# SwiGLU gate and up with the tokens held in the array and 512 weight columns streamed, on one Trainium2 core

## The chip, the core and the metric

The kernel runs as one program on one core of a Trainium2 chip. The metric is the device time of that core in microseconds, the median of several runs. PE is the matrix engine, DVE the vector engine, ACT the engine for activation functions, SP the queue that issues the loads. SBUF is the on-chip memory of 128 partitions in which an operand has a byte address within its partition; PSUM is the accumulator memory of eight banks of 512 float32 per partition.

## The reference, cut to what matters

Two layers of a decoder trunk on 256 tokens of width 2048, in float32. Layer 0 mixes by latent attention and a gated delta rule, layer 1 by RWKV-7 time mixing. Each mixer is followed by a SwiGLU network between two norms:

```
h = h + rms_norm(mixer(rms_norm(h)))
h = h + rms_norm(swiglu(rms_norm(h)))
swiglu(x) = (silu(x @ w_gate) * (x @ w_up)) @ w_down      # 2048 -> 5632 -> 2048
```

## The kernel before, in words

**Split products.** PE multiplies in a reduced-precision float32 type (fp32r), so every operand is split in two: `hi` is a rounded copy made by ACT and `lo` the rest, made by DVE (`split`, L268 to L270). A product is the sum of three matmuls, hi·hi, hi·lo and lo·hi (`mm3`, L311; the matmuls have the lines L313, L315 and L316 in the wide form, L313, L318 and L319 in the other).

**Weights** come from DRAM in chunks of 128 partitions × 1024 columns (two rows of blocks of 512 columns), 512 KB each, issued by SP at L367 into three buffers `raw`. Every chunk is split into `whi` and `wlo`, also with three buffers each (`wchunks`, L291).

**Two forms of a projection.** `proj_steps` (L338) holds a 128×128 block of the weight in the array and streams the 256 tokens past it; the output has channels on partitions. A chunk is 24 matmuls of 256 columns. `projT_steps` (L354) holds a block of 128 tokens of `x` in the array and streams 512 weight columns past it; the output has tokens on partitions. A chunk is 12 matmuls of 512 columns. Both fill two of four PSUM banks `pw` for 512 columns of a weight, so the next projection starts in the other two.

**SwiGLU** (`ffn`, L486) walks over 11 groups of 512 hidden channels, in parts of 4, 4 and 3 groups. In each group `proj` computes the gate and then `proj` the up product, eight chunks each. The evacuation of the gate multiplies by `rs` (the norm's reciprocal root of each token, spread over all partitions) on DVE (L504) and takes silu on ACT (L505); that of up multiplies by `rs` and by the gate on DVE (L509, L510) and splits the result into `hid_h` and `hid_l` (through L269 and L270), channels on partitions, which is the form that the down product needs. After each part `projT` with `hid` in the array and `w_down` streamed gives the output by token; `Out.evac` (L450) adds the parts up, and `Out.post` (L469) applies the post norm and adds to `h`.

**Order.** The instructions are laid out on the engines by a scheduler of the build, which takes an instruction when its inputs are there by its own timing; on the chip each engine then works through its list in that order. `weave` (L321) orders the work of the mixers by planned times.

**Where operands lie.** Tiles start on multiples of 32 bytes per partition: `epst` of 16 bytes and `hpi` of 4 bytes take 32 each. The pools lie in the order in which they are opened: `cp` (constants, `rs`, `junk`, small tiles), `wp` (`raw`, `whi`, `wlo`), `xt` (`xs_hi`, `xs_lo`: the split input of every projection), then those of the phases. In layer 0 the SwiGLU's tiles lie above two pools that layer 1 has closed by then: `rp` with 3,840 bytes of constants and `xn` with 16 × 257 × 4 = 16,448 bytes. The addresses in bytes:

| tile | in the array in | address | above a multiple of 256 |
|---|---|---|---|
| `whi`, first buffer (the others follow by 4,096) | the wide form | 36,096 | 0 |
| `xs_hi` (`xs_lo` 16,384 above) | `projT` of a mixer's output | 60,672 | 0 |
| `hid_h`, layer 1 (`hid_l` 20,480 above) | `projT` of `w_down` | 136,448 | 0 |
| `hid_h`, layer 0 (`hid_l` 20,480 above) | `projT` of `w_down` | 156,736 | 64 |
| `ch` (streamed only) | - | 195,424 | 96 |

Of the kernel before, what the change touches and what calls it, by code (L numbers as in the profile page):

```python
# [11 lines left out]
F32 = mybir.dt.float32  # L12
# [19 lines left out]
def doubling_masks(n):  # L32
    """-1 on the diagonal, 1 on the blocks below it that a doubling step joins."""
    i = np.arange(n)
    out = {}
    b = 1
    while b < n:
        blk = i // b
        m = ((blk[:, None] % 2 == 1) & (blk[None, :] == blk[:, None] - 1)) * 1.0 - np.eye(n)
        out[b] = m  # L40
        b *= 2
    return out
# [57 lines left out]
def tile_trunk(ctx: ExitStack, tc: tile.TileContext, A, out, dbg=None):  # L100
# [19 lines left out]
    class Scratch:  # L120
        """A pool of 1, 2 and 4 KB slots for one phase."""
# [23 lines left out]
    class Banks:  # L145
        """The eight PSUM banks: nw for projections, m under each other tag."""
# [41 lines left out]
    # ---------------------------------------------------------------- inputs and small parameters  # L188
# [42 lines left out]
    def params(pool):  # L231
        """the other parameters by channel"""
        pr = pool.tile([P, 3, P], F32, name="pr3")
        nc.gpsimd.memset(pr, 0.0)
        nc.gpsimd.dma_start(pr[0:96, 0, :], A["gdn_conv_w"][0].rearrange("j (c p) -> (j c) p", p=P))
        nc.gpsimd.dma_start(pr[96:100, 0, :], A["mla_q_norm"].rearrange("o (c p) -> (o c) p", p=P))
        nc.gpsimd.dma_start(pr[100:104, 0, :], A["mla_kv_norm"].rearrange("o (c p) -> (o c) p", p=P))
        nc.gpsimd.dma_start(pr[104:105, 0, :], A["gdn_out_norm"])
        nc.gpsimd.dma_start(pr[0:96, 1, :], A["rwkv_mix"][0].rearrange("j (c p) -> (j c) p", p=P))
        nc.gpsimd.dma_start(pr[96:112, 1, :], A["rwkv_w0"].rearrange("o (c p) -> (o c) p", p=P))  # L240
        nc.gpsimd.dma_start(pr[112:128, 1, :], A["rwkv_a0"].rearrange("o (c p) -> (o c) p", p=P))
        for i, n in enumerate(("rwkv_k_k", "rwkv_k_a", "rwkv_ln_w", "rwkv_ln_b")):
            nc.gpsimd.dma_start(pr[16 * i : 16 * i + 16, 2, :], A[n].rearrange("o (c p) -> (o c) p", p=P))
        nc.gpsimd.dma_start(pr[64:80, 2, :], A["rwkv_r_k"][0].rearrange("(c h) n -> c (h n)", h=2))
        yield 1
        tp = pbank("pB")
        for i in range(3):
            nc.tensor.transpose(out=tp[:, i * P : (i + 1) * P], in_=pr[:, i, :], identity=C("ident"))
            nc.vector.tensor_copy(prm[:, 1 + i, :], tp[:, i * P : (i + 1) * P])
        tsc(omka, prm[:, 3, 16:32], -1.0, 1.0, ALU.mult, ALU.add)  # L250
# [4 lines left out]
    # ---------------------------------------------------------------- helpers  # L255
# [6 lines left out]
    def behind(ins, first):  # L262
        """Has ins issued after an earlier instruction of its engine."""
        if first is not None:
            tc.add_manual_dep(ins.ins, first.ins.name, NOSYNC, reason="order")
        return ins
# [5 lines left out]
    # instructions of ACT and DVE that the splits of the next weights are not to delay  # L272
# [13 lines left out]
    def ahead(fill, kb, n, ncols):  # L286
        """Loads the rows that wchunks would load next."""
        early.append(wtiles(ncols))
        fill(early[-1][0], kb, n)

    def wchunks(fill, kbs, ncols, perm=None):  # L291
        """Loads and splits rows of a weight; yields (kb, hi, lo, first, last)."""
# [18 lines left out]
    def mm3(dst, lh, ll, rh, rl, start, stop, wide):  # L311
        """Three passes of the split product; wide: the first pair is the weight's."""
# [8 lines left out]
    def weave(tasks):  # L321
        """Emits the steps of generators (start, end, steps, generator, lead) in the order of their times;
        the lead is by how many instructions the scheduler takes them earlier."""
# [14 lines left out]
    def proj_steps(fill, kbs, ncols, xh, xl, evac, perm=None):  # L338
        """Columns of w^T x, channels on partitions: evac(i, [P, 2, T], tiles in it)."""
# [14 lines left out]
    def projT_steps(fill, kbs, xh, xl, evac):  # L354
        """512 columns of x w, tokens on partitions: evac(half, [P, 512])."""
# [17 lines left out]
    def rsq(v, n):  # L373
        """v^-1/2 of a few columns, by Newton steps from a guess by the exponent."""
# [11 lines left out]
    def rsq_table():  # L386
        """Has the table of the reciprocal root loaded before it is needed."""
        return act(tiny(1), epst[:, 0:1], AF.Abs_reciprocal_sqrt)

    def col_rs(ss, n):  # L390
        """Sums of squares [P, 2, parts] by token -> rsqrt(mean + eps) [P, 2]: the table's root and one Newton step."""
        v, m, r_ = tiny(2), tiny(2), tiny(2)
# [10 lines left out]
    def spread(col, dst, tag=None):  # L403
        """dst[:, t] = the column value of token t, on every partition."""
# [8 lines left out]
    rs = cp.tile([P, T], F32, name="rs")  # L413
    junk = cp.tile([P, 512], F32, name="junk")
# [8 lines left out]
    def feed(o, col0):  # L423
        """Four chunks of h: split parts of h*w, channels on partitions; its last instructions of ACT and DVE."""
# [15 lines left out]
    class Out:  # L440
        """Output of a sub-layer by token: times the post norm's weight, and its sums of squares."""
# [27 lines left out]
        def post(self, nxt):  # L469
            """h += rms(f) * w, 512 columns at a time."""  # L470
# [15 lines left out]
    def ffn(layer, nxt):  # L486
        """SwiGLU on the split x and its post norm; nxt as in post."""
        sc = Scratch(f"ffns{layer}", 3, 7, 1)
# [6 lines left out]
        for pi, ng in enumerate(parts):  # L495
            his, los = {}, {}
            for g in range(g0, g0 + ng):
                hid_h = fp.tile([P, 4, T], F32R, tag="hidh", name=nm("hidh"), bufs=5)
                hid_l = fp.tile([P, 4, T], F32R, tag="hidl", name=nm("hidl"), bufs=5)
                sg = S([P, 4, T], "sg")  # L500

                def ev_gate(b, ps, n):
                    gt = S([P, 2, T], "gt")
                    tt(gt, ps, bc2(rs, 2), ALU.mult)  # L504
                    act(sg[:, 2 * b : 2 * b + 2, :], gt, AF.Silu)  # L505

                def ev_up(b, ps, n):
                    ut = S([P, 2, T], "ut")
                    tt(ut, ps, bc2(rs, 2), ALU.mult)  # L509
                    tt(ut, ut, sg[:, 2 * b : 2 * b + 2, :], ALU.mult)  # L510
                    split(hid_h[:, 2 * b : 2 * b + 2, :], hid_l[:, 2 * b : 2 * b + 2, :], ut)

                proj(wfill(wg, g * 512, 512), KB, 512, xa(xs_hi), xa(xs_lo), ev_gate)
                proj(wfill(wu, g * 512, 512), KB, 512, xa(xs_hi), xa(xs_lo), ev_up)
# [13 lines left out]
    # ================================================================ layer 0: MLA + gated DeltaNet  # L528
# [45 lines left out]
    def gates():  # L574
        """beta, the log decays by token and their sums within the chunks of 128"""
# [13 lines left out]
        # log1p(u) = 2 atanh(u / (2 + u))  # L589
# [23 lines left out]
    def conv_bank(which, head0, ps):  # L613
        """causal conv of two heads from one PSUM bank"""
# [11 lines left out]
    def tok4(src, tag):  # L626
        """[P ch, (u, t)] -> PSUM bank [P tok, (c, u, ch)]"""
# [23 lines left out]
    # The key norms are folded: with k = s k^, T' = D^-1 T D for D = diag(s), and E = beta s^2 T' (v / s - e^g k S).  # L651
    def gdn_head(hq):
# [18 lines left out]
        # decay matrices [j, i]  # L671
# [40 lines left out]
    def gdn_solve(hq):  # L712
# [4 lines left out]
        # (I + M)^-1 by doubling its diagonal blocks: mt = -(I + M)^T, R = T^T  # L717
# [43 lines left out]
        # outputs by token; rms over the head with the query norm folded into its epsilon  # L761
# [25 lines left out]
    # ---- MLA  # L787
# [13 lines left out]
    def angles():  # L801
        """tables of the rotary embedding and the shared key"""
# [19 lines left out]
    def lora(i, col, scale):  # L822
        """Compressed q or kv: split parts of c * w and rsqrt of the mean square, by column and spread."""
# [132 lines left out]
    # in microseconds of the projections  # L956
# [45 lines left out]
    def mixer_out(w, fo, col0, kbs=KB, first=True):  # L1002
# [14 lines left out]
        spread(col_rs(ss, D), rs)  # L1017
# [13 lines left out]
    def turn(o):  # L1031
        """Four chunks of h times the norm's weight, channels on partitions; sums of squares by token."""
# [24 lines left out]
    # ================================================================ layer 1: RWKV-7  # L1057
# [16 lines left out]
    def normed(i, hi, lo):  # L1074
        """the normed input, its step from the token before, and the first mixture: a few channel tiles after another"""
# [37 lines left out]
    def lora32(i, w, slot, func):  # L1113
        """96 columns of w^T x in float32"""
# [29 lines left out]
    def low_rank(pr2):  # L1144
        """decay, in-context rate and gate of two channel tiles from the hidden low-rank parts"""
# [24 lines left out]
        # log decay, summed from the start of each chunk of 64  # L1170
# [23 lines left out]
    # in microseconds  # L1194
# [22 lines left out]
    # keys of two heads, block-diagonal  # L1217
# [20 lines left out]
    def headsum(dst, src, hi, lo):  # L1238
        """sums over the channels of a head, of the split src"""
# [4 lines left out]
    def rec_pre(pr2):  # L1244
        """receptance and key of two channel tiles"""
# [16 lines left out]
    def rec_head(pr2, j):  # L1262
# [4 lines left out]
        # 1 / |k|^2 by one Newton step (negated), times the inverse decay  # L1267
# [31 lines left out]
        # Gram matrices [s, t] of the two heads, one above the other  # L1299
# [14 lines left out]
        # values, centred over the head, in token layout  # L1314
# [8 lines left out]
        # decayed keys in token layout  # L1323
# [6 lines left out]
        # [(i, tokens), (chunk, head, channels)] -> tokens of a head under one another  # L1330
# [9 lines left out]
    def rec_solve(c):  # L1340
        j = c % 2
        pd, KR, AB, KG, V, BT, bon = heads.pop(c)
        # the last one is a chain of its own, in the slots of the heads
# [7 lines left out]
        # inverses of the unit triangular systems: two heads by four chunks  # L1351
# [18 lines left out]
        # chunk recurrence  # L1370
# [67 lines left out]
    # The output projection takes the channels that are done while the others are in the recurrence.  # L1438
# [29 lines left out]
    # in units of the time that two channel tiles take  # L1468
# [65 lines left out]
```

## Time and profile before

| what | value |
|---|---|
| median of 3 runs | 2735.04 us (2732.78 to 2735.78) |
| span of the profiled execution | 2731.1 us |
| its own whole time | not listed beside the runs; the span is 3.9 us under their median |
| instructions | 53510 |

A line of the page's fifth part or of the view by lines reads: line, engine, operation, output<-inputs (the streamed operand first, then the one held in the array), shapes, count | busy us, mean ns of one | idle time ahead and who ended it. A line of the timeline reads: start, length, engine, line, operation, and "xN" where N instructions are merged. Matmuls overlap, so the time that a matmul costs is the distance from one start to the next, not its length.

### The profile page before, as it was taken

The numbers are of one execution on the slowest core, as the hardware profiler recorded it, in microseconds if no ns is written. First come the engines' busy times: TensorE is split into PE (matmuls) and PEld (weight loads), VectorE is DVE, ScalarE is ACT, GpSimd is POOL, SyncE is SP. The second block draws the span as 40 slices with busy tenths as digits, with TensorE's granted clock in tenths as the row PEclk, the third lists the DMA queues.
The fourth block names the chain that finished last, engine by engine and source line by source line (L and its number), as shares of the span: only waits on it lengthen the run. The fifth ranks groups of instructions, "written<-read, shape, count | busy, mean of one in ns | idle before, by whom it ended". The sixth has DMA issues, their size and how long they took to land. (4 is left out here: it accounts for less than half of the span.)

```text
span 2731.1 us, 53510 instructions
## 1 busy us (share of the span) xinstructions
PE 2670.9 (98%) x22326; PEld 2482.5 (91%) x22326; DVE 1654.9 (61%) x2557; ACT 1347.4 (49%) x2113; POOL 35.9 (1%) x99
## 2 busy tenths in 40 slices
PE   8999999999999999998999999999799999999998
PEld 8999988899899989987999999977699989998996
DVE  7866566655445554557876676766755545555555
ACT  6655455544444443444576556554544444443443
POOL 1000000000000000000000000000000000000000
PEclk9999999999999999998999999999899999999999
DMA  7434545666666666665586333533266666666664
GB/s 213 140 109 116 161 141 194 183 182 183 188 185 183 185 185 185 185 185 178 166 279 207 106 117 116 169 123 99 88 180 184 186 193 184 183 188 193 182 182 161
DMA packets 281970, 462.07 MB, mean 169 GB/s; under 512 B 24488, under 2 KB 101728, under 8 KB 280960
## 3 DMA queue, kind: packets, MB, share of 16 engines
q1 hardware_dynamic: 281344, 458.50, 55.3%
q8 instruction: 174, 2.85, 0.4%
q14 instruction: 68, 0.56, 0.1%
q0 software_dynamic: 384, 0.16, 0.0%
HBM read 442.31 MB, written 16.29 MB: 168 GB/s over the span
## 5 line engine op out<-in xcount | busy, mean ns | idle before, releaser
L270 DVE TENSOR_TENSOR wlo<-raw,whi 128x1024 fp32r<-128x1024 f32 (+1 forms) x814 | 975.0, 1200 | 855.5 <-ACT whi L269 851.4
L269 ACT ACTIVATE whi<-raw 128x1024 fp32r<-128x1024 f32 (+1 forms) x814 | 843.9, 1039 | 1057.8 <-PE pw L315 682.0
L313 PE MATMUL pw<-xs_hi,whi 128*128 128x256 f32 x3984 | 1131.4, 285 | 4.3 <-ACT xs_hi L1095 3.6
L315 PE MATMUL pw<-xs_lo,whi 128*128 128x256 f32 x3984 | 1131.9, 285 | 0.0
L316 PE MATMUL pw<-xs_hi,wlo 128*128 128x256 f32 x3984 | 1127.7, 285 | 1.7 <-DVE wlo L270 1.6
L313 PEld LDWEIGHTS pw<-xs_hi,whi 128*128 128x128 f32 x3984 | 764.7, 192 | 6.5 <-ACT xs_hi L1095 3.9
L316 PEld LDWEIGHTS pw<-xs_hi,wlo 128*128 128x128 f32 x3984 | 762.5, 192 | 4.1 <-DVE wlo L270 2.5
L315 PEld LDWEIGHTS pw<-xs_lo,whi 128*128 128x128 f32 x3984 | 764.9, 192 | 1.5 <-DVE xs_lo L1085 0.3
L319 PE MATMUL pw<-whi,hidl 128*128 128x512 f32 x704 | 276.6, 393 | 0.0
L318 PE MATMUL pw<-wlo,hidh 128*128 128x512 f32 x704 | 275.8, 392 | 0.0
L313 PE MATMUL pw<-whi,hidh 128*128 128x512 f32 x704 | 248.6, 392 | 0.0
L319 PEld LDWEIGHTS pw<-whi,hidl 128*128 128x128 f32 x704 | 132.2, 188 | 30.1
L313 PEld LDWEIGHTS pw<-whi,hidh 128*128 128x128 f32 x704 | 132.3, 188 | 29.5
L318 PEld LDWEIGHTS pw<-wlo,hidh 128*128 128x128 f32 x704 | 132.3, 188 | 29.0
L313 PE MATMUL pw<-whi,xs_hi 128*128 128x512 f32 x256 | 103.0, 417 | 3.7 <-ACT xs_hi L269 3.5
L318 PE MATMUL pw<-wlo,xs_hi 128*128 128x512 f32 x256 | 105.0, 410 | 0.0
L319 PE MATMUL pw<-whi,xs_lo 128*128 128x512 f32 x256 | 101.7, 405 | 0.0
L316 PE MATMUL pw<-xr_hi,wlo 128*128 128x256 f32 x288 | 83.3, 289 | 2.8 <-DVE wlo L270 2.7
L313 PE MATMUL pw<-xr_hi,whi 128*128 128x256 f32 x288 | 83.3, 289 | 0.1
L315 PE MATMUL pw<-xr_lo,whi 128*128 128x256 f32 x288 | 82.6, 287 | 0.0
L313 PEld LDWEIGHTS pw<-whi,xs_hi 128*128 128x128 f32 x256 | 48.9, 193 | 15.4 <-ACT xs_hi L269 4.1
L318 PEld LDWEIGHTS pw<-wlo,xs_hi 128*128 128x128 f32 x256 | 49.5, 193 | 10.5 <-issue 0.7
(670 smaller groups left out, 2754.6 us busy)
## 6 DMA issues: line engine op xcount, KB each, us to landing
raw<-in_ffn_w_gate_dram SPq DMA_DIRECT2D x176, 512.0 KB, 3.8
raw<-in_ffn_w_up_dram SPq DMA_DIRECT2D x176, 512.0 KB, 4.3
raw<-in_ffn_w_down_dram SPq DMA_DIRECT2D x176, 512.0 KB, 4.1
raw<-in_hyb_w_in_dram SPq DMA_DIRECT2D x80, 512.0 KB, 3.6
raw<-in_hyb_w_out_dram SPq DMA_DIRECT2D x32, 512.0 KB, 3.8
raw<-in_rwkv_w_v_dram SPq DMA_DIRECT2D x32, 512.0 KB, 4.2
raw<-in_rwkv_w_r_dram SPq DMA_DIRECT2D x32, 512.0 KB, 4.1
raw<-in_rwkv_w_k_dram SPq DMA_DIRECT2D x32, 512.0 KB, 3.7
```

The source lines that it names most:

```text
L269: behind(act(hi, src, AF.Copy), after[0])
L270: behind(tt(lo, src, hi.bitcast(F32), ALU.subtract), after[1])
L313: mm(dst, lhsT=lh, rhs=rh, start=start, stop=False, skip_group_check=True)
L315: mm(dst, lhsT=lh, rhs=rl, start=False, stop=False, skip_group_check=True)
L316: mm(dst, lhsT=ll, rhs=rh, start=False, stop=stop, skip_group_check=True)
L318: mm(dst, lhsT=lh, rhs=rl, start=False, stop=False, skip_group_check=True)
L319: mm(dst, lhsT=ll, rhs=rh, start=False, stop=stop, skip_group_check=True)
```

## The change

Gate and up go through `projT`: `xs_hi` and `xs_lo` are held in the array in blocks of 128 tokens, and 512 weight columns are streamed. Their outputs then have tokens on partitions, so the norm's factor is a column `rc` of two values per partition and no longer a spread row: the gate's evacuation is one ACT instruction per token block (silu with `rc` as its scale, read from PSUM), that of up one DVE instruction (`hd` = up × `rc` × gate). Eight PE transposes of 128×128 float32 per group turn `hd` back to channels on partitions, into two PSUM banks of the tags `pA` and `pB`, from which the split into `hid_h` and `hid_l` reads. `mixer_out` writes the column `rc` in place of spreading it. `rc` is a new tile of 2 float32 per partition in the pool `cp`, between `rs` and `junk`. The scratch pool of the SwiGLU has eight slots of 2 KB in place of seven and one of 4 KB. The down product, its evacuation and all else keep their code.

```diff
-    def col_rs(ss, n):
-        v, m, r_ = tiny(2), tiny(2), tiny(2)
+    def col_rs(ss, n, out=None):
+        v, m, r_ = tiny(2), tiny(2), tiny(2) if out is None else out
...
     rs = cp.tile([P, T], F32, name="rs")
+    rc = cp.tile([P, 2], F32, name="rc")
     junk = cp.tile([P, 512], F32, name="junk")
...
-        sc = Scratch(f"ffns{layer}", 3, 7, 1)
+        sc = Scratch(f"ffns{layer}", 3, 8)
...
-                sg = S([P, 4, T], "sg")
-                def ev_gate(b, ps, n):
-                    gt = S([P, 2, T], "gt")
-                    tt(gt, ps, bc2(rs, 2), ALU.mult)
-                    act(sg[:, 2 * b : 2 * b + 2, :], gt, AF.Silu)
-                def ev_up(b, ps, n):
-                    ut = S([P, 2, T], "ut")
-                    tt(ut, ps, bc2(rs, 2), ALU.mult)
-                    tt(ut, ut, sg[:, 2 * b : 2 * b + 2, :], ALU.mult)
-                    split(hid_h[:, 2 * b : 2 * b + 2, :], hid_l[:, 2 * b : 2 * b + 2, :], ut)
-                proj(wfill(wg, g * 512, 512), KB, 512, xa(xs_hi), xa(xs_lo), ev_gate)
-                proj(wfill(wu, g * 512, 512), KB, 512, xa(xs_hi), xa(xs_lo), ev_up)
+                sg = [S([P, 512], "sg") for _ in range(2)]
+                tb = []
+                def ev_gate(b, ps):
+                    act(sg[b], ps, AF.Silu, scale=rc[:, b : b + 1])
+                def ev_up(b, ps):
+                    if not tb:
+                        tb.extend(pbank() for _ in range(2))
+                    hd = S([P, 512], "hd")
+                    stt(hd, ps, rc[:, b : b + 1], sg[b], ALU.mult, ALU.mult)
+                    for j in range(4):
+                        nc.tensor.transpose(out=tb[j // 2][:, j % 2 * T + b * P : j % 2 * T + (b + 1) * P],
+                                            in_=hd[:, j * P : (j + 1) * P], identity=C("ident"))
+                projT(wfill(wg, g * 512, 512), KB, xa(xs_hi), xa(xs_lo), ev_gate)
+                projT(wfill(wu, g * 512, 512), KB, xa(xs_hi), xa(xs_lo), ev_up)
+                for u in range(2):
+                    split(hid_h[:, 2 * u : 2 * u + 2, :], hid_l[:, 2 * u : 2 * u + 2, :], pair(tb[u]))
...
-        spread(col_rs(ss, D), rs)
+        col_rs(ss, D, rc)
```

## Rows read from the trace of the kernel before

**Rows 1.** The page, parts 1 and 2: PE's busy time, and its granted clock by slice.
```profile
PE 2670.9 (98%) x22326; PEld 2482.5 (91%) x22326; DVE 1654.9 (61%) x2557; ACT 1347.4 (49%) x2113; POOL 35.9 (1%) x99
PEclk9999999999999999998999999999899999999999
```

**Rows 2.** Stretches: gate and up in layer 0, down in layer 1 (us, busy times, clock, DMA).
```profile
524.00:684.00 160.00, 160.00 (x1336) 160.00 (x1335) 83.46 (x81) 67.95 (x71) 0.00 (x0) 1.00 0.63 184
2159.20:2240.90 81.70, 81.70 (x363) 67.63 (x361) 38.23 (x33) 35.11 (x37) 0.00 (x0) 1.00 0.62 193
```

**Rows 3.** Timeline of ACT, gate and up of layer 0: splits of the first and fifth of five chunks.
```profile
535.03 1.06 ACT L269 ACTIVATE whi<-raw 128x1024 fp32r<-128x1024 f32 x1 [1.82 <-PE pw L315]
...
546.55 1.06 ACT L269 ACTIVATE whi<-raw 128x1024 fp32r<-128x1024 f32 x1 [1.82 <-PE pw L315]
```

**Rows 4.** Timeline of PE, down of layer 1: the same matmul of chunks 1 and 31.
```profile
2159.07 0.61 PE L313 MATMUL pw<-whi,hidh 128*128 128x512 f32 x2
...
2240.67 0.61 PE L313 MATMUL pw<-whi,hidh 128*128 128x512 f32 x2
```

**Rows 5.** Timeline of PE, output projection of layer 0's mixer: the same matmul of two chunks.
```profile
484.38 0.62 PE L313 MATMUL pw<-whi,xs_hi 128*128 128x512 f32 x2
...
487.10 0.62 PE L313 MATMUL pw<-whi,xs_hi 128*128 128x512 f32 x2
```

**Rows 6.** Timeline of PE, down of layer 0: the same matmul of two chunks.
```profile
768.71 0.63 PE L313 MATMUL pw<-whi,hidh 128*128 128x512 f32 x2
...
771.51 0.63 PE L313 MATMUL pw<-whi,hidh 128*128 128x512 f32 x2
```

**Rows 7.** Timeline of PE, a projection with ch streamed: two starts 24 matmuls apart.
```profile
326.04 0.28 PE L316 MATMUL pw<-ch,wlo 128*128 128x256 f32 x1
...
328.92 0.28 PE L316 MATMUL pw<-ch,wlo 128*128 128x256 f32 x1
```

**Rows 8.** DMA issues of the two weights (count, size, us to landing).
```profile
raw<-in_ffn_w_gate_dram SPq DMA_DIRECT2D x176, 512.0 KB, 3.8
raw<-in_ffn_w_up_dram SPq DMA_DIRECT2D x176, 512.0 KB, 4.3
```

**Rows 9.** Line L313: matmuls by operand (count: ns min/median/max, first and last start, forms).
```profile
L313 PE MATMUL pw<-xs_hi,whi x3984: 276/283/581, 11.4 to 2652.6; 128*128 128x256 f32 x200
L313 PE MATMUL pw<-whi,hidh x704: 389/393/398, 684.7 to 2717.6; 128*128 128x512 f32 x176
L313 PE MATMUL pw<-xr_hi,whi x288: 274/281/470, 1329.3 to 1742.3; 128*128 128x256 f32 x144
L313 PE MATMUL pw<-whi,xs_hi x256: 387/392/796, 348.2 to 1957.1; 128*128 128x512 f32 x128
L313 PE MATMUL pw<-ch,whi x112: 277/281/472, 322.9 to 425.4; 128*128 128x256 f32 x112
L313 PE MATMUL pw<-wl,whi x64: 276/280/283, 1353.0 to 1406.9; 96*128 96x256 f32 x32, 128*128 128x256 f32 x32
```

**Rows 10.** Timeline of PE: one set of four transposes of layer 0.
```profile
89.71 0.60 PE L632 MATMUL pB<-cst,vT 128*128 128x128 f32 x4
```

**Rows 11.** Line L632: the lengths of these transposes (ns min/median/max).
```profile
L632 PE MATMUL pB<-cst,vT x16: 270/272/273, 89.7 to 229.3; 128*128 128x128 f32 x16
```

**Rows 12.** The page, part 5, and view by lines: splits and evacuations.
```profile
L270 DVE TENSOR_TENSOR wlo<-raw,whi 128x1024 fp32r<-128x1024 f32 (+1 forms) x814 | 975.0, 1200 | 855.5 <-ACT whi L269 851.4
L269 ACT ACTIVATE hidh<-ut 128x512 fp32r<-128x512 f32 x44 | 27.1, 633 | 8.5 <-DVE ut L510 8.5
L463 DVE TENSOR_TENSOR fw<-pw,fw 128x512 f32<-128x512 f32 x32 | 20.7, 682 | 10.7 <-PE pw L319 10.7
L478 DVE SCALAR_TENSOR_TENSOR hA<-fw,tiny,hA 128x512 f32<-128x512 f32 x16 | 10.9, 744 | 0.1
```

**Rows 13.** Timeline, spread of rs in layer 0: DVE's two instructions, PE's four.
```profile
514.36 0.48 DVE L407 TENSOR_SCALAR junk<-cst,tiny 128x128 f32<-128x128 f32 x2
517.71 0.60 PE L410 MATMUL pA<-junk,ones 128*128 128x128 f32 x4
```

## The prediction

> **What bounds the kernel now.** I read the page first: PE is busy for 98% of the span, and its clock is granted almost throughout [rows 1]. Then the table by stretches: in gate and up as in down, PE is busy for the whole stretch at a clock of 1.00, which is the 2.4 GHz level, while DVE and ACT are near half and the loads at 184 to 193 GB/s [rows 2]. So in these stages the time is the distance from one matmul start to the next, and the timelines give it per chunk of 512 KB. Gate and up: four chunks lie between the two splits of [rows 3], (546.55 − 535.03) / 4 = 2.88 us, or 0.120 us for each of 24 matmuls of 256 columns; the columns alone would take 256 / 2.4 GHz = 0.1067. Down in layer 1: thirty chunks in 81.60 us, 2.72 us each, or 0.2267 for each of 12 matmuls of 512 columns, whose columns take 0.2133 [rows 4]. The mixer's output projection, which holds `xs` in the array and streams weights as the change will, takes 2.72 too [rows 5]. So a matmul carries 13.3 ns (32 cycles of 2.4 GHz) beyond its columns in both forms, and wider ones pay it half as often. That is what the change can win.
>
> But down in layer 0 takes 2.80 us for the same chunk [rows 6], 6.7 ns (16 cycles) more for each matmul. Its weights, buffers, widths and clock are those of layer 1; what differs is the address of the operand in the array: by the table of addresses `hid` starts 64 bytes above a multiple of 256 in layer 0 and on one in layer 1. `whi` and `xs` lie on such multiples. The streamed operand doesn't matter in this way: `ch`, 96 above, is streamed at 24 matmuls in 2.88 us [rows 7]. I read it so: an operand held in the array off its boundary costs 16 cycles more per matmul.
>
> **What the change moves without meaning to.** `rc` takes a slot of 32 bytes in `cp`, ahead of `wp` and `xt`. So `whi`, `wlo`, `xs_hi`, `xs_lo` and `hid` of layer 1 all come to lie 32 above a multiple of 256, `hid` of layer 0 96 above (the scratch pool shrinks by 2,048, which changes nothing here). No row shows an operand held at 32. The bounds: nothing (13.3 ns as now) and 24 cycles, 10 ns, if the price goes with the bytes left to the next multiple of 128 (64 bytes cost 16 cycles, 96 then 24). Between them lie 8 cycles, if it goes with the bytes past the boundary, and 16, if any offset costs the same. I take the row that is nearest, 16 cycles, 6.7 ns [rows 6].
>
> **The sum, part by part.**
> - Gate and up: 176 + 176 chunks [rows 8]. From 2.88 us to 2.80: 352 × 0.08 = −28.2 us. (Without the offset 2.72: 352 × 0.16 = −56.3.)
> - Down in layer 1: of 704 matmuls at L313 [rows 9] half, four to a chunk, 88 chunks × 0.08 = +7.0. In layer 0 nothing, as it is off the boundary already.
> - All other projections that hold weights: of 3,984 matmuls at L313 with `xs` 352 × 8 = 2,816 are gate and up; 1,168 stay, and with 288, 112 and 64 of the other operands 1,632, times three passes 4,896 [rows 9]; × 6.67 ns = +32.6. I charge it in full, since PE is busy there too [rows 1].
> - The mixers' output projections: 256 × 3 = 768 matmuls [rows 9] × 6.67 ns = +5.1.
> - Transposes: 11 groups × 8 × 2 layers = 176. Four take 0.60 us in the trace [rows 10] and one is 0.27 long [rows 11], so (0.60 − 0.27) / 3 = 0.11 each: +19.4. They lie on PE, which has no gap to hide them.
> - The spread that goes: four float32 matmuls per layer at the same 0.11 [rows 13]: −0.9.
> - Evacuation: DVE loses three instructions of 128x512 per token block and gains one like L478, 0.744; the splits read PSUM, like L463, 0.68 [rows 12]. Lighter on an engine half idle: 0. If that cover went, the weights' splits would come late, by the 0.7 us of one such instruction at most per group, 15 in all.
> - Loads: the same bytes; at the fastest pace, 2.72 us a chunk, they ask for 193 GB/s, at which down runs without a wait [rows 2]: 0. SP and POOL get no new work.
> - A new wait: a transpose needs `hd`, and the next gate's matmuls stand behind it on PE. If the scheduler puts other matmuls in between, it costs nothing. If the transposes stand right behind up's last matmul, PE waits for two of 0.744 one after the other, less what it does meanwhile: about 0.5 us, and 1.7 if a weight's split of 1.2 us [rows 12] is ahead on DVE; 12 to 38 us over 22 groups. The one like case, PE's part of the spread, starts 2.9 us after DVE's ended [rows 13], so the scheduler leaves room. I take 0.1 us per group, +2; ends 0 and 38.
>
> Sum: −28.2 + 7.0 + 32.6 + 5.1 + 19.4 − 0.9 + 2 = **+37.0 us**. The profiled span of 2731.1 is 3.9 below the median of 2735.04, which I carry along: 2735.04 + 37.0 = **2772 us**.
>
> The Trainium skill speaks against the gain itself: "TensorE: Matmul & The Clock Gate", section "Back-to-back issue gap", gives columns / 2.4 GHz + 2.5 ns for a matmul. By that an estimate of a chunk is 2.62 us in the old form and 2.59 in the new one, and the gain 352 × 0.03 = 10.6 us, less than the transposes. The trace disagrees: 2.88 and 2.72 [rows 3, 4].
>
> **The rivals.**
> - **32 bytes cost nothing.** Then only the form counts: −56.3 + 19.4 − 0.9 + 2 = −35.8, **2699 us**, faster. It is decided in SBUF, by whether the boundary that [rows 6] shows bites at 32 too; it turns the sign below about 3.3 ns per matmul. For it: no row has an operand at 32. Against it: 64 costs 6.7 ns. The Trainium skill has it this way: "SBUF — State Buffer", section "Specifications (TRN2)", gives SBUF lines of 16 bytes, and 32 and 64 are both whole lines. By that rule 64 would cost nothing either, and [rows 6] differ from it.
> - **8 cycles, in step with the offset.** Gate and up at 2.76: −42.2, the three shifted terms halved, +22.4, `hid` of layer 0 +0 to +3.5, and +20.5 for the rest: +1 to +4, **2737 us**, no change.
> - **24 cycles.** 10 ns: gate and up 2.84, −14.1; +67.1 shifted; +20.5: +73.5, **2809 us**.
> - **PE waits for `hd`** and the offset is free: −37.8 + 12 to 38, **2709 to 2735 us**. For it: PE takes its list in order. Against it: no wait of PE stands in the stretches of [rows 2], and [rows 13].
> - **The form wins only 10 us**, as the formula above has it; on rows it would take a chunk of 2.85 in the new form, against 2.72 in [rows 5]: −10.6 + 20.5, **2745 us**.
>
> **How the numbers follow.** 16 cycles: 0.42. Free: 0.27. 8 cycles: 0.19. 24 cycles: 0.05. Waits: 0.05. Small win: 0.02. A measurement tells 0.2%, 5.5 us, from no change. Faster: the free case and most of the waits, 0.30. Same: most of the 8 cycles, 0.16. Slower: the rest, 0.54. The likeliest case alone runs from 2762 (if a third of the +32.6 is hidden in the recurrence) to 2784 (with 14 us of waits). The range must take in the free case and leaves out 24 cycles and the worst waits: **2694 to 2784**.
>
> **What would show it.** In the changed trace, gate and up at 2.80 us a chunk, down at 2.80 in both layers, and projections of weights outside the SwiGLU at 24 matmuls in 3.04 us instead of 2.88; 176 transposes 0.11 apart, and no wait of PE on `hd`. If chunks of gate and up take 2.72 and the others 2.88 as before, the offset is free and I am wrong on the sign. If PE waits on `hd` by a microsecond a group, the scheduler's room was the mistake.

## The result, and the profile after

The changed kernel takes **2696.7 us** (median of 4 runs, 2692.25 to 2702.23) against 2735.05 (2732.78 to 2735.78): ratio 0.986 [0.9846, 0.9875], 38 us or 1.4% faster. The forecast was 2772 and slower; the rival "32 bytes cost nothing" had 2699. The profiled run took 2699.26 us with a span of 2697.4.

The page of the changed kernel, parts 1 and 2, answers to [rows 1]:

```profile
PE 2633.5 (98%) x18270; PEld 2279.8 (85%) x18270; DVE 1602.1 (59%) x2465; ACT 1347.7 (50%) x2111; POOL 36.2 (1%) x99
...
PEclk9999999999999999998999999999899999999999
```

PE is the bound as before, with 4,056 matmuls fewer and the clock granted almost throughout. The table by stretches, as in [rows 2] (stretch, length, busy time of PE, PEld, DVE, ACT and POOL, clock, DMA share, GB/s): gate and up in layer 0, down in layer 0, down in layer 1.

```profile
530.00:546.00 16.00, 16.00 (x73) 13.23 (x71) 8.65 (x8) 6.37 (x6) 0.00 (x0) 1.00 0.66 197
762.00:778.00 16.00, 16.00 (x72) 13.11 (x71) 7.36 (x6) 7.29 (x8) 0.00 (x0) 1.00 0.67 194
2143.00:2225.00 82.00, 82.00 (x364) 67.89 (x363) 36.78 (x30) 36.56 (x39) 0.00 (x0) 1.00 0.63 192
```

PE has no gap in any of them at the 2.4 GHz level, and the loads of gate and up keep up at 197 GB/s. So the pace of the matmuls is again the time. The timeline of ACT in gate and up of layer 0, the splits of the first and fifth of five chunks, as in [rows 3]:

```profile
532.82 1.06 ACT L269 ACTIVATE whi<-raw 128x1024 fp32r<-128x1024 f32 x1 [1.66 <-PE pw L319]
...
543.70 1.06 ACT L269 ACTIVATE whi<-raw 128x1024 fp32r<-128x1024 f32 x1 [1.66 <-PE pw L319]
```

Four chunks in 10.88 us are **2.72 us** each: neither the old 2.88 nor the forecast 2.80. The timeline of PE gives the other projections, two rows each: `ch` streamed (as [rows 7]), the mixer's output (as [rows 5]), down in layer 0 (as [rows 6]) and down in layer 1 (as [rows 4]):

```profile
326.14 0.28 PE L316 MATMUL pw<-ch,wlo 128*128 128x256 f32 x1
...
328.96 0.28 PE L316 MATMUL pw<-ch,wlo 128*128 128x256 f32 x1
...
478.84 0.62 PE L313 MATMUL pw<-whi,xs_hi 128*128 128x512 f32 x2
...
487.00 0.62 PE L313 MATMUL pw<-whi,xs_hi 128*128 128x512 f32 x2
...
756.04 0.63 PE L313 MATMUL pw<-whi,hidh 128*128 128x512 f32 x2
...
764.44 0.63 PE L313 MATMUL pw<-whi,hidh 128*128 128x512 f32 x2
...
2145.34 0.62 PE L313 MATMUL pw<-whi,hidh 128*128 128x512 f32 x2
...
2180.70 0.62 PE L313 MATMUL pw<-whi,hidh 128*128 128x512 f32 x2
```

The 24 matmuls with `ch` take 2.82 us (2.88 before), three chunks of the mixer's output 8.16 (2.72 each, as before), three of down in layer 0 8.40 (2.80, as before), thirteen of down in layer 1 35.36 (2.72, as before). `whi`, `xs` and `hid` now lie 32 bytes further on, while `ch` keeps its place at 195,424; none of these became slower, and `ch` became quicker.

Where the time went shows in the same instruction of both kernels: the last split of down in layer 0, a split in layer 1's recurrence, and the last split of down in layer 1. From the timelines of DVE, first of before, then of after:

```profile
1252.12 1.23 DVE L270 TENSOR_TENSOR wlo<-raw,whi 128x1024 fp32r<-128x1024 f32 x1 [1.57 <-ACT whi L269]
...
1959.09 1.22 DVE L270 TENSOR_TENSOR wlo<-raw,whi 128x1024 fp32r<-128x1024 f32 x1
...
2711.44 1.23 DVE L270 TENSOR_TENSOR wlo<-raw,whi 128x1024 fp32r<-128x1024 f32 x1 [1.49 <-ACT whi L269]
```

```profile
1233.46 1.23 DVE L270 TENSOR_TENSOR wlo<-raw,whi 128x1024 fp32r<-128x1024 f32 x1 [1.57 <-ACT whi L269]
...
1943.31 1.22 DVE L270 TENSOR_TENSOR wlo<-raw,whi 128x1024 fp32r<-128x1024 f32 x1
...
2677.85 1.23 DVE L270 TENSOR_TENSOR wlo<-raw,whi 128x1024 fp32r<-128x1024 f32 x1 [1.49 <-ACT whi L269]
```

The distance is −18.7 us after layer 0, −15.8 in the recurrence and −33.6 at the end. So the SwiGLU of layer 0 gave 18.7 and that of layer 1 17.8 (at 496 us, in the output projection of layer 0's mixer, the two traces agree within 0.1 us); the mixer of layer 1 between them lost 2.9. In e8 below, which differs by a factor of 0.0 in layer 0 alone and has every tile at the same address, the three lie at 1234.19, 1939.65 and 2673.14: there the two SwiGLUs gave 17.9 and 18.9 and the mixer 1.5. So the mixer's part differs by some us from one execution to the next, and no price of the change is shown in it. By the terms of the prediction without the offset, a layer is worth 176 × 0.16 − 88 × 0.11 + 0.45 = 18.9 us.

The transposes, in the timeline of PE, between two matmuls of the next gate, and the instruction that they need, in the timeline of DVE:

```profile
548.04 0.39 PE L319 MATMUL pw<-whi,xs_lo 128*128 128x512 f32 x1
548.27 0.38 PE L513 MATMUL pA<-cst,hd 128*128 128x128 f32 x2
548.49 0.38 PE L513 MATMUL pB<-cst,hd 128*128 128x128 f32 x2
548.70 0.38 PE L513 MATMUL pA<-cst,hd 128*128 128x128 f32 x2
548.92 0.38 PE L513 MATMUL pB<-cst,hd 128*128 128x128 f32 x2
549.06 0.48 PE L313 MATMUL pw<-whi,xs_hi 128*128 128x512 f32 x1
549.37 0.40 PE L318 MATMUL pw<-wlo,xs_hi 128*128 128x512 f32 x1
```

```profile
543.22 1.40 DVE L511 SCALAR_TENSOR_TENSOR hd<-pw,rc,sg 128x512 f32<-128x512 f32 x2
```

From L319 at 548.04 to L318 at 549.37 are 1.33 us. The two matmuls of 512 columns in it take 2 × 0.2267, so eight transposes take 0.877, **0.110 us each**. `hd` is ready at 544.62, 3.65 us before the first of them (3.65 to 3.79 in all 22 groups): the scheduler put more than a chunk of the next gate in between, and the transposes wait for nothing.

### The profile page after: what moved, and what is told of

Its sections match the earlier page's. It is cut to its first block, busy times and chain, and to the rows that moved or that the text cites. A ratio compares the mean times of both kernels' runs of the same rounds, so it can differ in the third digit from the quotient of the medians.

```text
span 2697.4 us, 45270 instructions
## 1 busy us (share of the span) xinstructions
PE 2633.5 (98%) x18270; PEld 2279.8 (85%) x18270; DVE 1602.1 (59%) x2465; ACT 1347.7 (50%) x2111; POOL 36.2 (1%) x99
## 4 chain that ended last, share of the span: by engine, by line
PE 91%; DMA 3%; DVE 3%; ACT 2%; issue 1%; SPq 0%; DVEq 0%; ACTq 0%
PE pw L313 26%; PE pw L318 20%; PE pw L319 20%; PE pw L316 7%; PE pw L315 6%; PE ph L1312 1%; DMA raw<-in_rwkv_w_v_dram 1%; PE pA L1240 1%; PE pC L643 1%; PE pA L643 1%; PE pC L1240 1%; DVE wlo L270 1%; PE pB L1240 1%; DMA ygs<-bon 1%; ACT whi L269 1%
## 5 line engine op out<-in xcount | busy, mean ns | idle before, releaser
L318 PE MATMUL pw<-wlo,xs_hi 128*128 128x512 f32 x1664 | 653.2, 393 | 0.3 <-DVE wlo L270 0.3
L319 PE MATMUL pw<-whi,xs_lo 128*128 128x512 f32 x1664 | 648.8, 391 | 0.0
L313 PE MATMUL pw<-whi,xs_hi 128*128 128x512 f32 x1664 | 602.1, 395 | 6.0 <-ACT xs_hi L269 4.8
L313 PEld LDWEIGHTS pw<-whi,xs_hi 128*128 128x128 f32 x1664 | 313.8, 189 | 72.0 <-ACT xs_hi L269 5.3
L318 PEld LDWEIGHTS pw<-wlo,xs_hi 128*128 128x128 f32 x1664 | 314.3, 189 | 65.3 <-DVE wlo L270 0.7
L319 PEld LDWEIGHTS pw<-whi,xs_lo 128*128 128x128 f32 x1664 | 313.1, 188 | 65.5 <-issue 0.7
L313 PE MATMUL pw<-xs_hi,whi 128*128 128x256 f32 x1168 | 334.7, 288 | 4.8 <-ACT xs_hi L1100 3.6
L315 PE MATMUL pw<-xs_lo,whi 128*128 128x256 f32 x1168 | 335.5, 288 | 0.0
L316 PE MATMUL pw<-xs_hi,wlo 128*128 128x256 f32 x1168 | 331.4, 288 | 0.0
L319 PE MATMUL pw<-whi,hidl 128*128 128x512 f32 x704 | 276.5, 393 | 0.0
L318 PE MATMUL pw<-wlo,hidh 128*128 128x512 f32 x704 | 275.8, 392 | 0.0
L313 PE MATMUL pw<-whi,hidh 128*128 128x512 f32 x704 | 250.1, 393 | 0.0
L313 PEld LDWEIGHTS pw<-xs_hi,whi 128*128 128x128 f32 x1168 | 224.5, 193 | 6.4 <-ACT xs_hi L1100 3.8
L315 PEld LDWEIGHTS pw<-xs_lo,whi 128*128 128x128 f32 x1168 | 224.8, 192 | 1.3 <-DVE xs_lo L1090 0.3
L316 PEld LDWEIGHTS pw<-xs_hi,wlo 128*128 128x128 f32 x1168 | 222.6, 192 | 1.7 <-issue 0.7
L319 PEld LDWEIGHTS pw<-whi,hidl 128*128 128x128 f32 x704 | 132.2, 188 | 29.9
L313 PEld LDWEIGHTS pw<-whi,hidh 128*128 128x128 f32 x704 | 132.3, 188 | 29.5
L318 PEld LDWEIGHTS pw<-wlo,hidh 128*128 128x128 f32 x704 | 132.3, 188 | 29.1
L313 PE MATMUL pw<-xr_hi,whi 128*128 128x256 f32 x288 | 83.8, 291 | 1.4 <-ACT whi L269 1.4
```

The costliest lines, as they stand in the source:

```text
L313: mm(dst, lhsT=lh, rhs=rh, start=start, stop=False, skip_group_check=True)
L315: mm(dst, lhsT=lh, rhs=rl, start=False, stop=False, skip_group_check=True)
L316: mm(dst, lhsT=ll, rhs=rh, start=False, stop=stop, skip_group_check=True)
L318: mm(dst, lhsT=lh, rhs=rl, start=False, stop=False, skip_group_check=True)
L319: mm(dst, lhsT=ll, rhs=rh, start=False, stop=stop, skip_group_check=True)
```

## The experiments

All edits are made to the changed kernel. "Distance" is how far `xs`, `hid` or another operand made of tokens lies above the weight `whi` that it meets in a matmul, in bytes, modulo 256; in the form with 512 columns it is the held one and `whi` the streamed one. In the changed kernel `xs` and `hid` of layer 1 have distance 0, `hid` of layer 0 64, as in the kernel before; `rc` moved `whi` and all of them alike.

**e1: `whi`, `xs` and `hid` 32 bytes further** (absolute place against no price).

```diff
-    rc = cp.tile([P, 2], F32, name="rc")
+    rc = cp.tile([P, 16], F32, name="rc")[:, 0:2]
```

> The changed kernel with 32 bytes more ahead of the weight buffers: whi, wlo, xs and hid of layer 1 lie 64 above a multiple of 256, hid of layer 0 128 above. Theory A (an operand held in the array costs 16 cycles of 2.4 GHz more per matmul if it starts 64 to 127 above a multiple of 128, and nothing at 0 to 63): gate, up and down of layer 1 take 2.80 us a chunk in place of 2.72, the projections that hold weights 3.04 in place of 2.88, down of layer 0 falls from 2.80 to 2.72; in all +28.2 + 7.0 + 32.6 + 5.1 - 7.0 = +66 us on 2697, 2763. Rival B (the address is not the cause of the 2.80 us in layer 0): 2697, and down of layer 0 stays at 2.80.

Measured: 2698.36 us (2694.57 to 2700.5), ratio 0.9865 [0.985, 0.988]. In the timelines of e1, ACT in gate and up, then PE in down of layer 0:

```profile
533.53 1.06 ACT L269 ACTIVATE whi<-raw 128x1024 fp32r<-128x1024 f32 x1 [1.66 <-PE pw L319]
...
544.41 1.06 ACT L269 ACTIVATE whi<-raw 128x1024 fp32r<-128x1024 f32 x1 [1.66 <-PE pw L319]
...
756.76 0.63 PE L313 MATMUL pw<-whi,hidh 128*128 128x512 f32 x2
...
765.16 0.63 PE L313 MATMUL pw<-whi,hidh 128*128 128x512 f32 x2
```

`xs`, held at 64 above a multiple of 256, runs at 2.72; `hid` of layer 0, now at 128, still at 2.80. An absolute place sets neither. So the prediction's reading of [rows 6] fell, and it was open what makes layer 0 slow.

**e2: `hid` of layer 0 alone 32 bytes further.**

```diff
+        if not layer:
+            nc.gpsimd.memset(fp.tile([P, 8], F32, name="pad0"), 0.0)
```

> The changed kernel with a pad of 32 bytes ahead of hid in layer 0 alone, which then lies 128 above a multiple of 256. Theory A: down of layer 0 at 2.72 us a chunk, 88 chunks x 0.08 = -7 us on 2697, 2690. If the boundary is one of 256 bytes: 2.80 as before, 2697. Rival B: 2697.

Measured: 2695.35 us (2693.79 to 2697.7), ratio 0.9856 [0.9842, 0.9871]; down in layer 0 at 2.81 us a chunk. Its distance is now 96: still slow.

**e3: each transpose done twice** (their price).

```diff
-                    for j in range(4):
+                    for j in (0, 1, 2, 3, 0, 1, 2, 3):
```

> The changed kernel with each of the 176 PE transposes done twice. If a transpose costs PE 0.11 us and nothing hides it: +19.4 us on 2697, 2716. If transposes are hidden beside the loads of operands into the array or in waits: nearer to 2697. If a burst of transposes lowers the clock: more than 2716.

Measured: 2712.46 us (2709.18 to 2715.21), ratio 0.9914 [0.9898, 0.9931]. That is 15.8 us more than the changed kernel for 176 transposes, 0.09 us each; the runs of the two kernels spread over 6 and 10 us, so it does not contradict 0.110. In the trace of e3 the stretch from L319 to L318 around sixteen transposes takes 2.21 us (550.31 to 552.52) against 1.33 around eight: 0.110 each again.

**e4: the next projection's first matmuls ordered behind the transposes** (what the scheduler's room is worth). `mm3` returns its first matmul `m`, and `box["T"]` is the last transpose.

```diff
+                if first:
+                    behind(m, box.get("T"))
```

> The changed kernel with the first matmul of the projection after up ordered behind the last transpose on PE. If the room that the scheduler leaves hides the wait for hd: PE now waits 0.5 to 1.7 us in each of 22 groups, +12 to +38 us on 2697, 2709 to 2735. If the gated tokens are there in time anyway: 2697.

Measured: 2719.87 us (2717.2 to 2721.42), ratio 0.9944 [0.9929, 0.9959]: 23.2 us more, 1.05 per group. Two lines of e4's waits (who waited for whom: us in all, times, longest), and its PE timeline at one group:

```profile
PEld pA L516 <- DVE hd L514: 12.2, 24, 0.8
...
PEld pB L516 <- DVE hd L514: 10.1, 20, 0.8
```

```profile
543.49 0.39 PE L319 MATMUL pw<-whi,xs_lo 128*128 128x512 f32 x1
544.23 0.44 PE L516 MATMUL pA<-cst,hd 128*128 128x128 f32 x2 [0.35 <-DVE hd L514]
...
544.89 0.44 PE L516 MATMUL pA<-cst,hd 128*128 128x128 f32 x2
...
545.30 0.48 PE L313 MATMUL pw<-whi,xs_hi 128*128 128x512 f32 x1
```

The 22.3 us are waits of the weight loads (PEld), which partly lie beside the end of the matmul before. What PE itself loses stands in the starts: from L319 at 543.49 to L313 at 545.30 are 1.81 us, against 1.02 in the changed kernel (548.04 to 549.06), so 0.79 a group and 17 us in 22 groups, most of the loss; where the rest goes was not looked into. This wait is what the rival "PE waits for `hd`" described; it exists, and the order of the instructions avoids it.

**e5: `hid` of layer 0 brought to `whi`'s place** (distance 0).

```diff
+        if not layer:
+            nc.gpsimd.memset(fp.tile([P, 48], F32, name="pad0"), 0.0)
```

> The changed kernel with a pad of 192 bytes ahead of hid in layer 0, which then lies 288 above a multiple of 512, as hid of layer 1, whi and xs do. Theory C (the address counts within 512 bytes: 256 to 320 is free, 64 to 128 costs 16 cycles a matmul): down of layer 0 at 2.72 us a chunk, -7 us on 2697, 2690. Theory D (what differs is the layer, its data or its time, and no address): 2.80, 2697.

Measured: **2688.05 us** (2686.98 to 2691.3), ratio 0.9832 [0.9815, 0.9848]. PE in down of layer 0 of e5:

```profile
756.47 0.62 PE L313 MATMUL pw<-whi,hidh 128*128 128x512 f32 x2
...
761.91 0.62 PE L313 MATMUL pw<-whi,hidh 128*128 128x512 f32 x2
```

Two chunks in 5.44 us, 2.72 each: the slow layer is cured by 192 bytes of padding, for 8.7 us between the medians.

**e6: `hid` of layer 1 at the addresses of layer 0** (the place or something else in the layer).

```diff
+        if layer:
+            nc.gpsimd.memset(fp.tile([P, 5072], F32, name="pad1"), 0.0)
```

> The changed kernel with a pad of 20,288 bytes ahead of hid in layer 1, so that hid has the same addresses in both layers. Theory C, or any theory of the address: down of layer 1 goes from 2.72 us a chunk to 2.80, +7 us. Theory D: it stays at 2.72 and the time at 2697.

Measured: 2702.55 us (one run). PE in down of layer 1 of e6, eight chunks in 22.40 us, 2.80 each:

```profile
2161.35 0.63 PE L313 MATMUL pw<-whi,hidh 128*128 128x512 f32 x2
...
2183.75 0.63 PE L313 MATMUL pw<-whi,hidh 128*128 128x512 f32 x2
```

The price follows the address into the other layer. The end of this stage also tells whether the price comes from the other engines, which write and split weights beside `whi` while PE reads it. After the last split no engine but PE works and no transfer runs (stretch as in [rows 2]), and the same matmul of the last two chunks still starts 2.80 us apart:

```profile
2682.10:2687.30 5.20, 5.20 (x24) 4.20 (x23) 0.00 (x0) 0.00 (x0) 0.00 (x0) 1.00 0.00 0
...
2682.26 0.63 PE L313 MATMUL pw<-whi,hidh 128*128 128x512 f32 x2
...
2685.06 0.63 PE L313 MATMUL pw<-whi,hidh 128*128 128x512 f32 x2
```

**e7: `whi`, `xs` and `hid` all 320 bytes further than in the changed kernel**, 64 modulo 256 (their distances kept).

```diff
-    rc = cp.tile([P, 2], F32, name="rc")
+    rc = cp.tile([P, 88], F32, name="rc")[:, 0:2]
```

> The changed kernel with a pad of 320 bytes ahead of the weight buffers: whi, xs and hid of layer 1 lie 96 above a multiple of 512. Theory C: gate, up and down of layer 1 at 2.80 us a chunk, projections that hold weights at 3.04 in place of 2.88, in all about +73 us, 2770. Theory D: 2697.

Measured: 2697.3 us (one run); down at 2.80 in layer 0 and 2.72 in layer 1. With the kernel before, the changed one and e1 it is the fourth common place at which the form with 512 columns keeps its pace; the expectation's theory C, a price by the address within 512 bytes, fell with it.

**e8: zeros in `hid` of layer 0** (the data). In layer 0 `hd` is multiplied by 0.0, so that this layer's SwiGLU adds nothing.

```diff
-                    stt(hd, ps, rc[:, b : b + 1], sg[b], ALU.mult, ALU.mult)
+                    stt(hd, ps, rc[:, b : b + 1] if layer else 0.0, sg[b], ALU.mult, ALU.mult)
```

> The changed kernel with the gated product of layer 0 multiplied by zero, so that hid of layer 0 holds zeros (the SwiGLU of layer 0 is left out of the result; the instructions and addresses stay). If the 2.80 us of down in layer 0 come from the numbers in hid: 2.72 there, 2690. If not: 2.80, 2697.

Measured: 2694.51 us (one run), down in layer 0 still at 2.80. Values are not the cause.

**e9: `xs` 320 bytes further from `whi`** (does distance cost where `xs` is held, too).

```diff
+    nc.gpsimd.memset(xt.tile([P, 80], F32, name="pad0"), 0.0)
```

> The changed kernel with a pad of 320 bytes between the weight buffers and xs: seen from whi within 512 bytes, xs lies at 320 (it was at 0), hid at 128 in layer 0 (it was at 320) and at 320 in layer 1 (it was at 0). Theory R (what counts is where the operand held in the array lies as seen from the streamed one): gate and up at 2.80 us a chunk, +28.2; the mixers' output projections +5.1; down of layer 1 at 2.80, +7.0; down of layer 0 unknown, -7 to 0: about 2730 to 2737. If only hid's own place counts: down of layer 1 at 2.80 and gate and up at 2.72, 2697 to 2704.

Measured: 2722.15 us (2721.11 to 2722.6), ratio 0.995 [0.9933, 0.9967]: 25.5 us more than the changed kernel. Its timelines (line numbers one higher), ACT in gate and up, then PE in a projection of the wide form:

```profile
533.22 1.06 ACT L270 ACTIVATE whi<-raw 128x1024 fp32r<-128x1024 f32 x1 [1.74 <-PE pw L320]
...
544.42 1.06 ACT L270 ACTIVATE whi<-raw 128x1024 fp32r<-128x1024 f32 x1 [1.74 <-PE pw L320]
...
326.45 0.28 PE L314 MATMUL pw<-xs_hi,whi 128*128 128x256 f32 x1
...
327.81 0.28 PE L314 MATMUL pw<-xs_hi,whi 128*128 128x256 f32 x1
```

Gate and up take 2.80 (11.20 / 4), the very figure of the forecast, and down in layer 1 too (its distance is 64 now, 128 in layer 0). That is 352 × 0.08 + 88 × 0.08 = +35 us in the SwiGLU, and +5 in the mixers' output projections, which take 2.80 as well: 15 more than the whole run lost. The second pair tells where some came back: 12 matmuls of the wide form in 1.36 us, 0.113 us each in this stretch. Over the whole span the wide matmuls with `xs` lie 0.1175 us apart in place of 0.1196 (as in the table of e13 to e16); for 3,504 of them that is 7 us. The rest stays open.

**e10, e11, e12: the map of distances** (`hid` alone is moved, in both layers).

```diff
+        nc.gpsimd.memset(fp.tile([P, A if layer else B], F32, name="pad0"), 0.0)
```

with A and B 16 and 112 in e10, 8 and 80 in e11, 48 and 160 in e12.

> The changed kernel with hid at 256 (layer 0) and 64 (layer 1) as seen from whi within 512 bytes. If the distance counts within 128 bytes: down at 2.72 us a chunk in layer 0 and 2.80 in layer 1, 2697. If the price lies in a part of the 512 bytes around 320 to 352: 64 is free, and 256 tells where that part begins: 2690 to 2697.

> The changed kernel with hid at 128 (layer 0) and 32 (layer 1) as seen from whi. If the distance counts within 128 bytes: 2.72 in layer 0, and 32 costs 0 to 16 cycles in layer 1: 2690 to 2697. If in 512 bytes around 320: both free, 2690.

> The changed kernel with hid at 448 (layer 0) and 192 (layer 1) as seen from whi. If the distance counts within 128 bytes, both are 64 off: 2.80 in both layers, 2704. If in 512 bytes around 320: 192 free, 448 unknown, 2690 to 2697.

Measured, one run each: 2697.65, 2702.82 and 2691.9 us. PE in down of layer 0 of e12, two chunks in 5.49 us, 2.75 each:

```profile
754.79 0.62 PE L313 MATMUL pw<-whi,hidh 128*128 128x512 f32 x2
...
760.28 0.62 PE L313 MATMUL pw<-whi,hidh 128*128 128x512 f32 x2
```

Two forecasts missed: at 128 (e11) a period of 128 bytes would have given 2.72, and 192 (e12) fits neither 2.80 nor a free place.

All runs together, for a chunk of 12 matmuls with 512 columns streamed:

| distance of the held operand from `whi`, modulo 256 | us a chunk | seen in |
|---|---|---|
| 0 | 2.72 | before, after, e1, e5, e7, e10 (layer 0, at 256) |
| 32 | 2.80 | e11 (layer 1) |
| 64 | 2.80 | before, after, e1, e6, e7, e8, e9 (gate and up), e10 (layer 1) |
| 96 | 2.81 | e2 |
| 128 | 2.79 | e9, e11 (layer 0) |
| 192 | 2.75 | e12 (both layers) |

**e13 to e16: the wide form's weights moved by themselves** (its term, +32.6, was the largest wrong one, and no run had moved it alone). On top of e5; the form with 512 columns keeps using the part of the tile at 0; `off` is 48, 32, 16 and 8, or 192, 128, 64 and 32 bytes.

```diff
-    def wtiles(ncols):
+    def wtiles(ncols, off=48):
...
-        whi = wp.tile([P, CH], F32R, tag="whi", name=nm("whi"), bufs=3)
-        wlo = wp.tile([P, CH], F32R, tag="wlo", name=nm("wlo"), bufs=3)
+        whi = wp.tile([P, CH + 64], F32R, tag="whi", name=nm("whi"), bufs=3)[:, off : off + CH]
+        wlo = wp.tile([P, CH + 64], F32R, tag="wlo", name=nm("wlo"), bufs=3)[:, off : off + CH]
```

> Edit, on top of the best version so far (hid of layer 0 brought to whi's place modulo 256, 2688.05 us): each weight tile whi and wlo is 256 bytes longer, and the wide form uses the part that starts 192 bytes in, while the form that streams 512 columns still uses the part at 0. So in the wide form alone the streamed xs lies 64 bytes (modulo 256) from the held weight, the distance that it had when xs was moved by 320. Theory (the wide form's price goes with the distance too, and 64 is cheaper than 0): starts of wide matmuls 0.114 to 0.118 us apart in place of 0.120; 4,896 of them by 2 to 3 ns, 10 to 14 us less: 2674 to 2678 us, gate, up and down still 2.72 a chunk. Rival (the wide form's quicker pace in that run came from elsewhere, as from the slower SwiGLU): 2686 to 2691 us, starts 0.120. Reading of the prediction (an offset of the held operand costs 16 cycles in the wide form as well): +32.6, 2721 us.

> As the run with 192, but the wide form's weights start 128 bytes in: the streamed operand at 128 from the held one. Theory (price by distance): between 2674 and 2690 us, since no wide row at 128 was seen yet (ch at 96 bytes took 0.118 to 0.120); another pace than at 64. Rival (distance doesn't count in the wide form): 2686 to 2691. Reading of the prediction: 2721.

> As the run with 192, but 64 bytes in: the streamed operand at 192 (modulo 256) from the held one. Theory (price by distance): another pace than at 0; on the other form 192 cost less than 64, so if the wide form's gain is the mirror of that loss, a smaller gain than at 64: 2680 to 2688 us. Rival (distance doesn't count in the wide form): 2686 to 2691. Reading of the prediction: 2721.

> As the run with 192, but 32 bytes in, the very offset that the prediction charged with 16 cycles, here between the two operands of the wide form (streamed at 224 modulo 256 from the held one). Theory (price by distance): between 2674 and 2690 us. Rival (distance doesn't count in the wide form): 2686 to 2691. Reading of the prediction: +32.6, 2721 us.

Measured, with the mean time between neighbouring starts of wide matmuls that stream `xs` or `xr` (an operand of layer 1's mixer), over the whole span of each trace; starts more than 0.13 us apart are left out, and the distance in bytes, as defined above, stands in brackets:

| run | us | ratio to before | `xs` | `xr` |
|---|---|---|---|---|
| e5 (0) | 2688.05 (2686.98 to 2691.3) | 0.9832 [0.9815, 0.9848] | 0.1196 (0) | 0.1159 (192) |
| e13 (192) | 2684.2 (2681.39 to 2686.55) | 0.9811 [0.9796, 0.9826] | 0.1175 (64) | 0.1195 (0) |
| e14 (128) | 2687.29 (2683.74 to 2693.37) | 0.9825 [0.9808, 0.9843] | 0.1187 (128) | 0.1173 (64) |
| e15 (64) | 2683.58 (2680.19 to 2685.39) | 0.9805 [0.9789, 0.9822] | 0.1155 (192) | 0.1187 (128) |
| e16 (32) | 2684.15 (2683.07 to 2686.89) | 0.9813 [0.9798, 0.9827] | 0.1183 (224) | 0.1179 (160) |

`xr` lies at 196,576 in every kernel here, as `ch` keeps 195,424; only `whi` moves against it. By distance the two columns are one map: 0 gives 0.1196 and 0.1195, 64 0.1175 and 0.1173, 128 0.1187 in both, 192 0.1155 and 0.1159. In the kernel before, where `xr` is at 224, it takes 0.1183, as `xs` does in e16. Twenty-four matmuls with `xr` in the timelines of PE, first in e5, then in e13:

```profile
1451.15 0.28 PE L313 MATMUL pw<-xr_hi,whi 128*128 128x256 f32 x1
...
1453.87 0.28 PE L313 MATMUL pw<-xr_hi,whi 128*128 128x256 f32 x1
```

```profile
1444.69 0.28 PE L313 MATMUL pw<-xr_hi,whi 128*128 128x256 f32 x1
...
1447.57 0.28 PE L313 MATMUL pw<-xr_hi,whi 128*128 128x256 f32 x1
```

They take 2.72 us at 192 and 2.88 at 0. The timelines of PE at the start of layer 1's mixer, nine matmuls with `xs` apart, first in the changed kernel, then in e15:

```profile
1269.59 0.28 PE L313 MATMUL pw<-xs_hi,whi 128*128 128x256 f32 x1
...
1270.67 0.28 PE L313 MATMUL pw<-xs_hi,whi 128*128 128x256 f32 x1
```

```profile
1269.18 0.28 PE L313 MATMUL pw<-xs_hi,whi 128*128 128x256 f32 x1
...
1270.20 0.28 PE L313 MATMUL pw<-xs_hi,whi 128*128 128x256 f32 x1
```

1.08 us against 1.02, 0.120 against 0.113 each. So distance counts in the wide form too, but there 0 is the slowest: an offset makes `xs` cheaper by 1 to 4 ns a matmul, and no offset costs 16 cycles. The 10 to 14 us that e13's expectation gave were too many: `xs` wins 7 us (3,504 × 2.1 ns) and `xr` loses 3 (864 × 3.6 ns), and the median lies 4 us under e5's. For e15 the same sum is 12 us and the medians differ by 4.5; where the rest goes was not found. All four medians lie 1 to 4.5 us under e5's, with intervals that overlap. e15 has the lowest median of all versions; its four runs lie below e5's, but whether it beats e5 is not settled. Both beat the changed kernel: none of their runs reaches its 2692.25 to 2702.23.

## Why the prediction was wrong

**The step that failed** is the reading of [rows 6]: "an operand held in the array off its boundary costs 16 cycles more per matmul", and with it the choice of "the row that is nearest, 16 cycles" for an operand at 32. The rows were right and the size too: 2.80 against 2.72 is real, and e9 brought it to gate and up. But what counts is the distance between the held and the streamed operand, not the place of the held one. In the kernel before, `whi` lay on a multiple of 256, so the two could not be told apart from the address of `hid`. `rc`, however, moves `whi`, `xs` and `hid` by the same 32 bytes, which leaves the distances among them as they were. By distance, the same rows give no change outside gate and up, save for `ch` and `xr`: they stay in place, so the moved `whi` takes `ch` from 96 to 64 and `xr` from 224 to 192, and both became quicker.

Term by term:
- Gate and up: forecast 352 × 0.08 = −28.2. Measured 2.72 a chunk, 352 × 0.16 = −56.3: the value that the prediction had in brackets. 28.2 us of the miss.
- Down in layer 1, forecast +7.0: measured 0, as it stays at 2.72.
- The wide form, forecast +32.6: `ch` runs at 2.82 instead of 2.88, the mean of `xs` went from 0.1199 to 0.1196, that of `xr` from 0.1183 to 0.1158, and e13 to e16 show that an offset doesn't cost there. Measured 0 or slightly below.
- The mixers' output projections, forecast +5.1: measured 0 (2.72).
- These four add to 72.9 us, and 2772 − 72.9 = 2699 is the rival that came true; it stands 2.4 us from the median.
- Transposes at 0.11, +19.4: right (0.110 in the traces of the changed kernel and of e3, 0.09 by e3's medians). The spread that goes, −0.9, was not measured by itself.
- Evacuation and loads at 0: right; PE has no gap in the stretches, and the loads run at 192 to 197 GB/s.
- The wait for `hd`, +2 with ends 0 and 38: 0 in the trace. The argument that the scheduler leaves room held, with 3.65 us at the group shown; without that room the kernel takes 23 us more (e4), inside the bounds.
- Down in layer 0, "nothing, as it is off the boundary already": the number was right, its reason not.

The result lies in the range of 2694 to 2784, near its lower end, because the range was made to take in this rival. Its chance of 0.27 was too low: the one row against it, 64 bytes at 6.7 ns, tells of 32 only if the price goes with the held operand's own place, and no row showed that. The streamed `ch`, 96 bytes off at no extra time [rows 7], was used for the streamed operand alone; it could as well have warned that an offset need not cost. And its reading, that the streamed operand's place doesn't matter, was wrong too: at 64 `ch` takes 2.82.

The Trainium skill, "SBUF — State Buffer", section "Specifications (TRN2)", gives SBUF lines of 16 bytes. By that rule all the distances tried, which are whole lines, would run alike; the trace agrees for a common shift (e1, e7) and differs for distances (2.72 to 2.81). By the formula of the Trainium skill, "TensorE: Matmul & The Clock Gate", section "Back-to-back issue gap", an estimate is that gate and up would win 10.6 us; that section gives it for a matmul by itself, not for a stream that loads a block for each, and the trace differs, with 56.3.

## What to carry to other kernels

When one stage of a kernel runs slower than its twin, compare the places of the two operands that a matmul reads, against each other and modulo 256 bytes, before blaming one of them; a pad of some hundred bytes is a cheap trial (here 8.7 us). A new small tile ahead of the big pools moves all of them alike and leaves their distances; it changes those to operands that keep their place, as `ch` and `xr` do here. And a transposition back on PE costs its 0.11 us a block and nothing more as long as other matmuls fill the time until its input is there.

## What the runs showed of the hardware

Not expected was that the pace of a stream of fp32r matmuls depends on how far apart the held and the streamed operand lie, with a period of 256 bytes. With 512 columns of weights streamed, 0 is best and 32 to 128 cost 6 to 7.5 ns a matmul. With 256 columns streamed past weights it is the other way: 0 is the slowest distance seen (0.120 us) and 192 the quickest (0.1155 to 0.116), the same for `xs` and for `xr`. With 512 columns the price stays when no other engine works and no transfer runs (e6), so no collision with the splits or the loads makes it. The period was seen at 256 (e10) and with 64 against 320 and 192 against 448 only. What in the chip makes it, and why the two forms differ, was not tried.
